# Convolution of the recurrent layer in four blocks of up to 344 tokens in place of five of 256, its runs dealt unevenly over the groups of the recursion

## The chip, the cores and the metric

The kernel runs on one core of a Trainium2 chip. The core has a matrix engine (PE, with its weight loads listed as PEld), a vector engine (DVE), an activation engine (ACT), a general engine (POOL) and an engine that only issues transfers (SP). Each engine takes its instructions in the order in which they were written down for it, and an instruction that waits holds up all that stand behind it on that engine. Data moves between DRAM, the on-chip memory and the accumulators in PSUM; a transfer is issued by an engine, most often SP, and lands some microseconds later.

The metric is the time of one execution on the device in microseconds (us), as a median of several runs. Each profile is of one execution.

## The reference, cut to what matters

The program is a backbone of two layers over 1024 latent tokens and 256 context tokens, 1024 features each. The even layer is the one that matters here. Its mixer has two halves of 512 features: a short gated convolution, and a recurrence (RWKV-7) that runs over the tokens in both directions.

```python
def conv3(u, w):
    up = jnp.pad(u, ((0, 0), (1, 1), (0, 0)))
    return up[:, :-2] * w[0] + up[:, 1:-1] * w[1] + up[:, 2:] * w[2]

def conv_branch(u, gate_b, gate_c):
    return gate_b * conv3(gate_c * u, conv_w)

def step(S, inp):                      # one token of the recurrence
    rt, wt, kt, vt, kkt, at = inp
    sa = jnp.einsum('bhij,bhj->bhi', S, -kkt)
    S = S * wt[:, :, None, :] + sa[..., None] * (kkt * at)[:, :, None, :] + vt[..., :, None] * kt[:, :, None, :]
    return S, jnp.einsum('bhij,bhj->bhi', S, rt)

p_lat = _split(h_lat @ w_in, EVEN_SPLIT)     # u, gate_b, gate_c: three projections of 512 features for the convolution
out_lat = jnp.concatenate([conv_branch(*p_lat[0:3]), rwkv_readout(...)], axis=-1) @ w_out
```

The convolution sees three neighbouring tokens; the context and the latent tokens are padded apart. So it is, in the main, three matrix products of (1280 tokens x 1024) by (1024 x 512), followed by a few elementwise operations.

## The kernel before

The work runs in stages, one after the other: the norm and projections of the even layer, the recursion of the recurrence with the convolution woven into it (`even_scan`), the output projection, an expert stage, the odd layer and a second expert stage. The change lies in the recursion's stage, with one edit in the stage ahead of it.

**Tokens in the recursion.** The 1280 tokens are cut into 20 pieces of 64, two pieces to a group, so there are ten groups, 0 to 9, and both directions advance together. For each group the kernel runs four generators, each of which issues some instructions and yields:

- `preps`, two groups ahead: loads of the inputs (tiles `s`, `ln`, `lr`, `lb`, `lk`), exponentials on ACT, products on DVE (tiles `AR`, `BK`), products on PE into `pr` (line 724, transposes line 738), which DVE masks into `PB` (line 728). Part of `PB` is stored to DRAM as `Ld` (line 735).
- `inverse`, one group ahead: loads `iW` from `Ld` (line 747) and runs 62 DVE operations in turn (lines 756 and 760, tiles `itmp` and `iG`); then it stores `iG` to DRAM as `Gd` in eight transfers (line 766) and loads it in another layout as `TT` in four (line 773).
- `merge`: DVE transposes `TT` into `Z` (line 782); PE multiplies twice (lines 788 and 796), with ACT copies between. The first of these products, `pu<-Z,PB` on line 788, is called the merge below.
- `serials`: two recursion steps for the two pieces of 64. PE products `X<-UV,PB` (line 819), `X<-S,AR` (826), `pu<-X,TT` (839), `pu<-UV,BT` (847), with ACT copies between, and the update of the state `S` on DVE (849, 850). A step needs the state of the one before.

**The convolution** (`conv`) is a fifth generator. For every block of 256 tokens it loads the split inputs `cvhh` and `cvhl` (line 626, one buffer each, so a block's load waits for the last product of the block before). For each of four feature blocks f it makes the three projections. A projection is two chunks; a chunk is one weight load `cvw` of 512 KB (line 641, three buffers) and 12 products of 256 columns (line 643), and then a yield. So a block has 24 chunks and the whole convolution 120. After the three projections of a feature block, ACT, DVE and POOL apply the gate and the three taps (tiles `cvu`, `cvg`, `cvx`, lines 634 to 658). What the next block needs of its left neighbour is kept in `keep`.

**What sets the order.** Each group's generators are dealt out by `interleave`, each with a number of runs and the stretch of the group in which they fall. The convolution has `NCV` = 10 runs in each of the twelve turns (-2 to 9). That is the order in which instructions are written; a scheduler in the language then places them on each engine by its own estimate of when they can start, so that a chunk may move to a place well ahead of its turn. The 12 products of a chunk are mostly kept together (`burst`).

**Ahead of the recursion** `keep()` in `even_project` stores the split inputs to DRAM (`hTD`), block by block, alternating with transfers of another generator.

Of the kernel before, what the change touches and what calls it, by code (L numbers as in the profile page):

```python
# [22 lines left out]
LT = LC + LL  # L23
# [30 lines left out]


N0, N2, N3 = 101, 1.0, .5
NCV = 10
NA = 4


# [120 lines left out]
class Kern:  # L181
# [252 lines left out]
    def even_project(self):  # L434
        nc, tc, I = self.nc, self.tc, self.I
        W = I["ev_w_in"][0]
        dp = self.dp
# [5 lines left out]
        with ExitStack() as es:  # L443
            P = lambda n, b, **k: es.enter_context(tc.tile_pool(name=n, bufs=b, **k))
            pp = P("pp", 3, space=PSUM)
            p2 = P("pp2", 2, space=PSUM)
            wp, hp = P("w", 2, side="right"), P("hT", 1, side="right")
            hT = [hp.tile([128, 8, LT], FR, name="hT" + x) for x in "hl"]
            with ExitStack() as e2:
                P2 = lambda n, b, **k: e2.enter_context(tc.tile_pool(name=n, bufs=b, **k))  # L450
                xp, sp, aw, ar = P2("hx", 4), P2("hs", 4), P2("haw", 3), P2("har", 2)
                self.even_hidden(hT, xp, sp, aw, ar, p2, P2("hps", 2, space=PSUM))
            self.hTD = [dp.tile([LT // 256, 128, 8, 256], FR, name="hTD" + x) for x in "hl"]

            def keep():
                for b in range(LT // 256):
                    for i in range(2):
                        nc.sync.dma_start(self.hTD[i][b].bitcast(FT), hT[i][:, :, b * 256:(b + 1) * 256].bitcast(FT))
                        yield

            p3 = P("pp3", 2, space=PSUM)
# [155 lines left out]
    def conv(self, P):  # L617

        nc = self.nc
        hp, wp, cp, c1, pp = P("cvh", 1), P("cvw", 3), P("cvt", 2), P("cv1", 1), P("cvp", 1, space=PSUM)  # L620
        keep = c1.tile([128, 4, 3], FT, name="keep")
        yield
        for b in range(LT // 256):
            h = [hp.tile([128, 8, 256], FR, name="cvh" + x) for x in "hl"]
            for i in range(2):
                nc.sync.dma_start(h[i].bitcast(FT), self.hTD[i][b].bitcast(FT))
            if b < 2:
                nc.gpsimd.memset(keep, 0.0)
            for f in range(4):

                u = cp.tile([128, 259], FT, name="cvu", bufs=1)
                g = cp.tile([128, 257], FT, name="cvg", bufs=1)
                t = cp.tile([128, 257], FT, name="cvx", bufs=1)
                nc.gpsimd.tensor_copy(u[:, 0:2], keep[:, f, 0:2])
                nc.gpsimd.tensor_copy(g[:, 0:1], keep[:, f, 2:3])
                nc.gpsimd.memset(u[:, 258:259], 0.0)
                for i, dst in enumerate((u[:, 2:258], g[:, 1:257], None)):
                    ps = pp.tile([128, 256], FT, name="cvp")
# [8 lines left out]
                    if dst is not None:  # L647
                        nc.scalar.activation(dst, ps, AF.Copy)
                nc.vector.tensor_tensor(u[:, 2:258], u[:, 2:258], ps, OP.mult)
                cw = lambda i: self.pcv("conv", 1, 4 * i + f)  # L650
                nc.scalar.activation(t, u[:, 0:257], AF.Copy, scale=cw(0))
                for i in (1, 2):
                    nc.vector.scalar_tensor_tensor(t, u[:, i:i + 257], cw(i), t, op0=OP.mult, op1=OP.add)
                nc.vector.tensor_tensor(t, t, g, OP.mult)
                x, y = (1 if b < 2 else 0), (257 if b in (0, LT // 256 - 1) else 256)
                nc.sync.dma_start(self.mixD[f, :, 256 * b - 1 + x:256 * b - 1 + y], t[:, x:y])
                nc.gpsimd.tensor_copy(keep[:, f, 0:2], u[:, 256:258])
                nc.gpsimd.tensor_copy(keep[:, f, 2:3], g[:, 256:257])

    def even_scan(self, P0):  # L660

# [8 lines left out]
        with es:  # L670
# [201 lines left out]
            for g in range(-2, NG):  # L872
                jobs = [(n, a, b, f(q)) for n, a, b, f, q in
                        ((2, 0.25, 0.4, merge, g), (4, 0.45, 1.2, serials, g), (15, 0.1, 1.05, inverse, g + 1),
                         (10, -0.3, 0.65, preps, g + 2)) if 0 <= q < NG]
                jobs.append((NCV, 0.0, 1.0, islice(conv, NCV)))
                if g > 7:

                    n = 31 if g == 8 else 10
                    jobs.append((n, 0.0, 1.0, islice(readout, n)))  # L880
                interleave(jobs)
# [1018 lines left out]
```

## Time and profile before

| | us |
|---|---|
| median of 3 runs | 4136.39 (4134.12 to 4136.67) |
| the profiled execution | 4126.59 |
| its span, first to last instruction | 4124.8 |
| recursion's stage, first convolution product to first output projection | 357 to 951 |
| mean granted PE clock over the span | 0.938 of full speed |

The page of the profile gives the busy time of each engine; the windows give the same for stretches of the span, with the granted PE clock as a share of full speed (2.4 GHz; the lower level is 1.2 GHz, 0.5 of it). The timeline gives single instructions with the idle time of the engine just before and what ended it. The chain of what ended last could be followed back only as far as 2347 us in this trace, so the recursion's stage has to be read from waits, windows and timeline.

Both timelines and windows count from the span's start. The first product of each merge stands at 456.6, 501.0, 548.9, 602.5, 650.2, 702.2, 753.1, 803.4, 853.8 and 909.9 us.

### The profile page before, as it was taken

The page shows a single profiled execution, that of the slowest core. Times are in us where ns is not written, and L with a number is a line of the kernel's source. Part 1 is how long each engine was busy: PE and PEld are TensorE (multiplying, and loading weights), DVE is VectorE, ACT ScalarE, POOL GpSimd, SP SyncE. Part 2 cuts the span into 40 slices and gives each one's busy share as a digit, 9 for nine tenths or more (in the row PEclk, how much of TensorE's full clock was granted, in tenths as well). Part 3 has the DMA queues.
Part 4 walks back from the last instruction along what each step waited for, and adds up shares of the span by engine and source line. Part 5 has one row for each costly group of instructions (what it writes and reads, how often), then busy time and mean ns, then how long its engine had stood idle before and what let it go on. Part 6 is the DMA issues. An engine that isn't in the chain of part 4 may idle for free. (4 is left out here: it accounts for less than half of the span.)

```text
span 4124.8 us, 66207 instructions
## 1 busy us (share of the span) xinstructions
PE 3737.1 (91%) x25578; PEld 2852.8 (69%) x25578; DVE 2764.9 (67%) x3906; ACT 2162.9 (52%) x3058; POOL 695.6 (17%) x682
## 2 busy tenths in 40 slices
PE   7989787868789999999999798998799499999998
PEld 5757787757556666666666565787467388888887
DVE  4255666764468777777777641465554599999997
ACT  4422222222246666666666431453555288878876
POOL 2101111242211010101010311452421210001010
PEclk9999899979889999999999899998799699999999
DMA  8988877756558787887878536223432699999997
GB/s 278 330 249 282 250 246 225 232 165 217 194 195 308 263 305 283 285 300 269 298 273 291 166 118 187 84 83 118 128 115 81 236 373 379 377 380 380 380 382 249
DMA packets 674650, 1026.25 MB, mean 249 GB/s; under 512 B 97089, under 2 KB 285537, under 8 KB 672542
## 3 DMA queue, kind: packets, MB, share of 16 engines
q1 hardware_dynamic: 657790, 963.22, 67.9%
q0 software_dynamic: 11360, 39.92, 3.7%
q10 hardware_dynamic: 5184, 18.88, 1.2%
q8 instruction: 201, 3.29, 0.3%
q14 instruction: 115, 0.94, 0.1%
HBM read 906.29 MB, written 115.60 MB: 248 GB/s over the span
## 5 line engine op out<-in xcount | busy, mean ns | idle before, releaser
L348 DVE TENSOR_TENSOR wl<-w,wh 128x1024 fp32r<-128x1024 f32 x1140 | 1356.0, 1221 | 134.9 <-ACT wh L347 105.4
L347 ACT ACTIVATE wh<-w 128x1024 fp32r<-128x1024 f32 x1152 | 1213.4, 1060 | 307.5 <-PE p L1115 251.5
L1115 PE MATMUL p<-wh,xh 128*128 128x512 f32 x1536 | 612.5, 399 | 0.0
L1115 PE MATMUL p<-wl,xh 128*128 128x512 f32 x1536 | 601.2, 391 | 0.2
L1115 PE MATMUL p<-wh,xl 128*128 128x512 f32 x1536 | 600.4, 391 | 0.0
L1115 PEld LDWEIGHTS p<-wh,xh 128*128 128x128 f32 x1536 | 289.6, 189 | 71.0 <-issue 13.4
L1115 PEld LDWEIGHTS p<-wl,xh 128*128 128x128 f32 x1536 | 289.3, 188 | 63.1 <-DVE wl L348 1.0
L1115 PEld LDWEIGHTS p<-wh,xl 128*128 128x128 f32 x1536 | 289.8, 189 | 57.2 <-DVE xl L348 0.4
L1115 PE MATMUL p<-wh,hh 128*128 128x512 f32 x768 | 307.9, 401 | 0.0
L1115 PE MATMUL p<-wl,hh 128*128 128x512 f32 x768 | 300.0, 391 | 0.3 <-DVE wl L348 0.2
L1115 PE MATMUL p<-wh,hl 128*128 128x512 f32 x768 | 299.8, 390 | 0.0
L353 PE MATMUL pj<-hTh,wchh 128*128 128x512 f32 (+1 forms) x720 | 279.2, 388 | 2.0 <-ACT wchh L347 1.1
L353 PE MATMUL pj<-hTl,wchh 128*128 128x512 f32 (+1 forms) x720 | 273.5, 384 | 5.2 <-DVE hTl L348 3.4
L353 PE MATMUL pj<-hTh,wchl 128*128 128x512 f32 (+1 forms) x720 | 276.9, 385 | 0.5 <-DVE wchl L348 0.5
L643 PE MATMUL cvp<-cvhh,cvw 128*128 128x256 f32 x960 | 207.2, 315 | 59.1 <-DMA cvw<-cwD 42.4
L643 PEld LDWEIGHTS cvp<-cvhh,cvw 128*128 128x128 f32 x960 | 165.1, 211 | 70.7 <-DMA cvw<-cwD 43.9
L1125 PE MATMUL pc<-w,xc 128*32 128x512 f32 x1536 | 174.7, 595 | 0.0
L1115 PEld LDWEIGHTS p<-wh,hh 128*128 128x128 f32 x768 | 144.1, 188 | 42.5 <-issue 13.4
L1115 PEld LDWEIGHTS p<-wl,hh 128*128 128x128 f32 x768 | 144.2, 188 | 32.7 <-DVE wl L348 1.1
L353 PEld LDWEIGHTS pj<-hTh,wchh 128*128 128x128 f32 x720 | 138.2, 192 | 38.8 <-issue 10.1
L353 PEld LDWEIGHTS pj<-hTl,wchh 128*128 128x128 f32 x720 | 136.6, 191 | 39.6 <-issue 10.8
L1115 PEld LDWEIGHTS p<-wh,hl 128*128 128x128 f32 x768 | 144.4, 188 | 27.8
(417 smaller groups left out, 6335.9 us busy)
## 6 DMA issues: line engine op xcount, KB each, us to landing
w<-in_moe_w_dram SPq DMA_DIRECT2D x576, 1024.0 KB
cvw<-cwD SPq DMA_DIRECT2D x120, 512.0 KB
adaw<-in_ada_w_dram SPq DMA_DIRECT2D x80, 512.0 KB
wch<-in_od_w_in_dram SPq DMA_DIRECT2D x38, 512.0 KB
cwD<-cvs SPq DMA_DIRECT2D x24, 512.0 KB
bias<-in_rpbt_dram SPq DMA_DIRECT2D x48, 192.0 KB
xt<-in_x_dram SPq DMA_DIRECT2D x16, 512.0 KB
adaw<-in_ada_w_dram SPq DMA_DIRECT2D x8, 1024.0 KB
```

Source lines behind the costliest of these rows:

```text
L347: self.nc.scalar.activation(hi, src, AF.Copy)
L348: (eng or self.nc.vector).tensor_tensor(lo, src, hi.bitcast(FT), OP.subtract)
L353: self.nc.tensor.matmul(ps, a[x], b[y], start=start and i == 0, stop=stop and i == 2, **kw)
L643: self.burst((lambda k=k, i=i, x=x, y=y: nc.tensor.matmul(ps, hl[:, x, k], h[y][:, k0 + k], start=k0 + k == 0 and i == 0, stop=k0 + k == 7 ...
L1115: self.keep(nc.tensor.matmul(ps[i], a[u], w[0][k][v], start=first and k == 0 and j == 0, stop=last and k == 3 and j == 2))
L1125: self.keep(nc.tensor.matmul(pc[32 * g:32 * g + 32], x[2][:, kt + kk, :], ws[g % 2][1][:, kk], start=n == 0 and k == 0, stop=n == len(stag ...
```

## The change

The blocks become (start, tokens) = (0, 256), (256, 344), (600, 344), (944, 336). The weight chunks stay as they are, so there are 96 in place of 120, and a product has 344 or 336 columns in place of 256 except in the context block. The runs per turn become six in the first five turns, seven in the next five, then 12 and 19. The small copies between blocks go from POOL to ACT and DVE and are made only where a next block needs them.

```diff
-NCV = 10
+NCV = [6] * 5 + [7] * 5 + [12, 19]
+CB = ((0, 256), (256, 344), (600, 344), (944, 336))
...
-            self.hTD = [dp.tile([LT // 256, 128, 8, 256], FR, name="hTD" + x) for x in "hl"]
+            self.hTD = [[dp.tile([128, 8, n], FR, name=f"hTD{x}{b}") for b, (_, n) in enumerate(CB)] for x in "hl"]
...
-                        nc.sync.dma_start(self.hTD[i][b].bitcast(FT), hT[i][:, :, b * 256:(b + 1) * 256].bitcast(FT))
+                        nc.sync.dma_start(self.hTD[i][b].bitcast(FT), hT[i][:, :, b0:b0 + n].bitcast(FT))
...
-        for b in range(LT // 256):
-            h = [hp.tile([128, 8, 256], FR, name="cvh" + x) for x in "hl"]
+        for b, (b0, n) in enumerate(CB):
+            h = [hp.tile([128, 8, big], FR, name="cvh" + x)[:, :, :n] for x in "hl"]
...
+            first, last = b < 2, b in (0, len(CB) - 1)
...
-                nc.gpsimd.tensor_copy(u[:, 0:2], keep[:, f, 0:2])
-                nc.gpsimd.tensor_copy(g[:, 0:1], keep[:, f, 2:3])
-                nc.gpsimd.memset(u[:, 258:259], 0.0)
+                nc.scalar.activation(u[:, 0:2], keep[:, f, 0:2], AF.Copy)
+                nc.scalar.activation(g[:, 0:1], keep[:, f, 2:3], AF.Copy)
+                if last:
+                    nc.gpsimd.memset(u[:, n + 2:n + 3], 0.0)
...
+                    elif i == 1:
+                        nc.scalar.activation(g[:, 1:n + 1], ps, AF.Copy)
+                        if not last:
+                            nc.scalar.activation(keep[:, f, 2:3], g[:, n:n + 1], AF.Copy)
...
-                nc.gpsimd.tensor_copy(keep[:, f, 0:2], u[:, 256:258])
-                nc.gpsimd.tensor_copy(keep[:, f, 2:3], g[:, 256:257])
+                if not last:
+                    nc.vector.tensor_copy(keep[:, f, 0:2], u[:, n:n + 2])
...
-                jobs.append((NCV, 0.0, 1.0, islice(conv, NCV)))
+                jobs.append((NCV[g + 2], 0.0, 1.0, islice(conv, NCV[g + 2])))
```

Line numbers in the changed kernel are higher by 5 to 10 in these functions (643 becomes 648, 788 becomes 798).

Three places show how the order of the engines changes. The first is SP's queue around the load of `TT` for group 3: `cvw` are the convolution's weights, `iW`, `Gd` and `TT` belong to the inverse, `yD` to a recursion step. Before:

```order
L641 DMA cvw<-cwD 128x1024
L747 DMA iW<-Ld 64x1024
L766 DMA Gd<-iG 16x16x32 x8
L773 DMA TT<-Gd 32x16x32 x4
L747 DMA iW<-Ld 64x1024
L694 DMA ln<-nkD 128x512
L694 DMA lr<-rD 128x512
L694 DMA ln<-nkD 128x512
L694 DMA lr<-rD 128x512
L656 DMA mixD<-cvx 128x256
L641 DMA cvw<-cwD 128x1024 x3
```

And in the changed kernel:

```order
L646 DMA cvw<-cwD 128x1024
L757 DMA iW<-Ld 64x1024
L776 DMA Gd<-iG 16x16x32 x8
L783 DMA TT<-Gd 32x16x32 x2
L866 DMA yD_2854<-Y 64x512
L866 DMA yD_2855<-Y 64x512
L783 DMA TT<-Gd 32x16x32 x2
L757 DMA iW<-Ld 64x1024
L822 DMA UV_5627<-vD 64x512
L822 DMA UV_5628<-vD 64x512
L646 DMA cvw<-cwD 128x1024 x3
```

In both, the weights for the next chunks stand behind the stores and loads of the inverse; before, 62 of the 120 weight loads are issued ahead of this `TT`, now 53 of the 96.

The second place is PE at a boundary between blocks of the convolution, where the first products of a new block need the inputs just loaded. Before, the boundary that stands at a merge is the one into the fourth block, at the merge of group 4:

```order
L738 MATMUL pr<-cst,BK 128x128 x4
L826 MATMUL X_6697<-S,AR 64x64 x2
L724 MATMUL pr<-AR,BK 128x128 x8
L643 MATMUL cvp<-cvhh,cvw 128x256 x2
L788 MATMUL pu<-Z,PB 32x32 x32
L724 MATMUL pr<-AR,BK 128x128 x8
L796 MATMUL pu<-TT,Z 32x32
L643 MATMUL cvp<-cvhl,cvw 128x256
```

In the changed kernel it is the one into the third block, ahead of the merge of group 2. The chunk's first two products stand ahead of products of the recursion and of `pr`, and of these rows the second begins the other ten products, which also stand ahead of the merge:

```order
L648 MATMUL cvp<-cvhh,cvw 128x344 x2
...
L734 MATMUL pr<-AR,BK 128x128 x7
...
L648 MATMUL cvp<-cvhl,cvw 128x344
...
L748 MATMUL pr<-cst,BK 128x128 x8
...
L798 MATMUL pu<-Z,PB 32x32 x32
L734 MATMUL pr<-AR,BK 128x128 x8
```

Before, two products of the new block are ahead of that merge, in the changed kernel all 12.

The third place is PE at the start of the ninth merge (group 8) before, with the chunks of the convolution beside it:

```order
L643 MATMUL cvp<-cvhl,cvw 128x256
L788 MATMUL pu<-Z,PB 32x32 x32
L724 MATMUL pr<-AR,BK 128x128 x8
L643 MATMUL cvp<-cvhh,cvw 128x256 x2
```

And the merge of group 7 in the changed kernel, after which no product of the convolution comes any more:

```order
L734 MATMUL pr<-AR,BK 128x128 x7
L798 MATMUL pu<-Z,PB 32x32 x32
L734 MATMUL pr<-AR,BK 128x128
L806 MATMUL pu<-TT,Z 32x32
L734 MATMUL pr<-AR,BK 128x128 x7
```

Counted on PE, the chunks that stand ahead of the merges of groups 0 to 9 are 30, 42, 52, 65, 72, 83, 95, 105, 116 and 120 before, and 29, 40, 49, 58, 70, 76, 88, 96, 96 and 96 in the changed kernel. The scheduler has moved the runs that the table deals to the last two turns to places ahead of the merge of group 7.

## Rows read from the trace of the kernel before

**Rows 1.** The page: busy time, share of the span, instructions; then one issue group.

```profile
PE 3737.1 (91%) x25578; PEld 2852.8 (69%) x25578; DVE 2764.9 (67%) x3906; ACT 2162.9 (52%) x3058; POOL 695.6 (17%) x682
...
cvw<-cwD SPq DMA_DIRECT2D x120, 512.0 KB
```

**Rows 2.** Windows: busy us (count) per engine, PE clock, DMA share, GB/s.

```profile
357.00:453.80 96.80, 77.91 (x683) 69.36 (x682) 62.30 (x152) 20.20 (x40) 13.08 (x43) 0.90 0.90 291
...
453.80:803.00 349.20, 291.83 (x5039) 267.40 (x5038) 227.32 (x642) 98.00 (x205) 53.34 (x158) 0.92 0.77 236
...
803.00:853.80 50.80, 41.11 (x654) 36.42 (x653) 36.40 (x90) 14.01 (x29) 20.00 (x31) 0.87 0.76 225
853.80:909.90 56.10, 36.90 (x616) 30.78 (x616) 39.73 (x90) 14.14 (x30) 22.64 (x23) 0.71 0.49 132
```

**Rows 3.** Waits, 350 to 950 us: waited for; total us, times, longest.

```profile
POOL cvu L634 <- DVE cvx L653: 31.2, 12, 5.5
...
PE cvp L643 <- DMA cvw<-cwD: 42.4, 22, 6.2
...
PE cvp L643 <- DMA cvhh<-hTDh: 12.7, 3, 8.8
```

**Rows 4.** Timeline of SP ahead of one merge: start, us, what.

```profile
727.70 3.42 SPq L766 DMA_DIRECT2D Gd<-iG  x7
731.22 3.27 SPq L773 DMA_DIRECT2D TT<-Gd  x4
...
737.78 0.88 SPq L641 DMA_DIRECT2D cvw<-cwD  x2
```

**Rows 5.** Timeline of DVE and PE at the same merge, idle time before in brackets.

```profile
726.00 0.19 DVE L760 TENSOR_TENSOR iG<-iG,itmp 128x16 f32<-128x16 f32 x1
...
743.64 0.79 PE L643 MATMUL cvp<-cvhh,cvw 128*128 128x256 f32 x2 [5.44 <-DMA cvw<-cwD]
745.09 0.63 PE L643 MATMUL cvp<-cvhh,cvw 128*128 128x256 f32 x2
...
745.73 0.63 PE L643 MATMUL cvp<-cvhh,cvw 128*128 128x256 f32 x2
...
753.15 1.04 PE L788 MATMUL pu<-Z,PB 32*32 32x32 f32 x54
...
753.25 0.69 DVE L728 TENSOR_TENSOR PB<-pr,cst 128x512 f32<-128x512 f32 x1 [8.04 <-PE pr L724]
```

**Rows 6.** Timeline of PE: products of 256 and of 512 columns in a stream.

```profile
361.17 0.40 PE L643 MATMUL cvp<-cvhh,cvw 128*128 128x256 f32 x2
...
361.53 0.40 PE L643 MATMUL cvp<-cvhh,cvw 128*128 128x256 f32 x2
...
350.98 0.40 PE L353 MATMUL pj<-hTh,wchh 128*128 128x512 f32 x1
351.21 0.39 PE L353 MATMUL pj<-hTh,wchl 128*128 128x512 f32 x1
```

**Rows 7.** Timeline of SP and PE at a block boundary, and at an earlier one.

```profile
641.84 0.43 SPq L626 DMA_DIRECT2D cvhh<-hTDh  x1
642.31 0.46 SPq L626 DMA_DIRECT2D cvhl<-hTDl  x1
...
649.44 0.80 PE L643 MATMUL cvp<-cvhh,cvw 128*128 128x256 f32 x2 [8.77 <-DMA cvhh<-hTDh]
...
654.26 0.58 PE L643 MATMUL cvp<-cvhl,cvw 128*128 128x256 f32 x1
```

**Rows 8.** Windows of the convolution's own instructions (`cvp`) alone, same columns.

```profile
803.00:853.80 50.80, 22.14 (x134) 19.67 (x132) 0.84 (x2) 1.54 (x4) 0.87 0.76 225
853.80:909.90 56.10, 8.06 (x48) 7.14 (x48) 0.42 (x1) 0.39 (x1) 0.71 0.49 132
```

**Rows 9.** Timeline of DVE and PE in the last groups, idle time before in brackets.

```profile
834.60 0.69 DVE L917 TENSOR_REDUCE m<-lr 128x8 f32<-128x512 f32 x1 [4.99 <-POOL lr L914]
...
909.93 1.92 PE L788 MATMUL pu<-Z,PB 32*32 32x32 f32 x64 [10.37 <-DVE Z L782]
```

More of the change, by code (lines that the diff above doesn't have):

```diff
@@ L619, in conv @@
         nc = self.nc
-        hp, wp, cp, c1, pp = P("cvh", 1), P("cvw", 3), P("cvt", 2), P("cv1", 1), P("cvp", 1, space=PSUM)
+        hp, wp, cp, c1, pp = P("cvh", 1), P("cvw", 3), P("cvt", 1), P("cv1", 1), P("cvp", 1, space=PSUM)
         keep = c1.tile([128, 4, 3], FT, name="keep")
+        big = max(n for _, n in CB)
         yield
-        for b in range(LT // 256):
-            h = [hp.tile([128, 8, 256], FR, name="cvh" + x) for x in "hl"]
+        for b, (b0, n) in enumerate(CB):
+            h = [hp.tile([128, 8, big], FR, name="cvh" + x)[:, :, :n] for x in "hl"]
             for i in range(2):
                 nc.sync.dma_start(h[i].bitcast(FT), self.hTD[i][b].bitcast(FT))
-            if b < 2:
+            first, last = b < 2, b in (0, len(CB) - 1)
+            if first:
                 nc.gpsimd.memset(keep, 0.0)
             for f in range(4):
-                u = cp.tile([128, 259], FT, name="cvu", bufs=1)
-                g = cp.tile([128, 257], FT, name="cvg", bufs=1)
-                t = cp.tile([128, 257], FT, name="cvx", bufs=1)
-                nc.gpsimd.tensor_copy(u[:, 0:2], keep[:, f, 0:2])
-                nc.gpsimd.tensor_copy(g[:, 0:1], keep[:, f, 2:3])
-                nc.gpsimd.memset(u[:, 258:259], 0.0)
-                for i, dst in enumerate((u[:, 2:258], g[:, 1:257], None)):
-                    ps = pp.tile([128, 256], FT, name="cvp")
+                u = cp.tile([128, big + 3], FT, name="cvu")
+                g = cp.tile([128, big + 1], FT, name="cvg")
+                t = cp.tile([128, big + 1], FT, name="cvx")
+                nc.scalar.activation(u[:, 0:2], keep[:, f, 0:2], AF.Copy)
+                nc.scalar.activation(g[:, 0:1], keep[:, f, 2:3], AF.Copy)
+                if last:
+                    nc.gpsimd.memset(u[:, n + 2:n + 3], 0.0)
+                for i in range(3):
+                    ps = pp.tile([128, big], FT, name="cvp")[:, :n]
                     for k0 in (0, 4):
@@ L646, in conv @@
                         yield
-                    if dst is not None:
-                        nc.scalar.activation(dst, ps, AF.Copy)
-                nc.vector.tensor_tensor(u[:, 2:258], u[:, 2:258], ps, OP.mult)
+                    if i == 0:
+                        nc.scalar.activation(u[:, 2:n + 2], ps, AF.Copy)
+                    elif i == 1:
+                        nc.scalar.activation(g[:, 1:n + 1], ps, AF.Copy)
+                        if not last:
+                            nc.scalar.activation(keep[:, f, 2:3], g[:, n:n + 1], AF.Copy)
+                nc.vector.tensor_tensor(u[:, 2:n + 2], u[:, 2:n + 2], ps, OP.mult)
+                m = n + last
                 cw = lambda i: self.pcv("conv", 1, 4 * i + f)
-                nc.scalar.activation(t, u[:, 0:257], AF.Copy, scale=cw(0))
+                nc.scalar.activation(t[:, :m], u[:, 0:m], AF.Copy, scale=cw(0))
                 for i in (1, 2):
[L653 to L656, printed above, removed]
-                nc.gpsimd.tensor_copy(keep[:, f, 0:2], u[:, 256:258])
-                nc.gpsimd.tensor_copy(keep[:, f, 2:3], g[:, 256:257])
+                    nc.vector.scalar_tensor_tensor(t[:, :m], u[:, i:i + m], cw(i), t[:, :m], op0=OP.mult, op1=OP.add)
+                nc.vector.tensor_tensor(t[:, :m], t[:, :m], g[:, :m], OP.mult)
+                x = 1 if first else 0
+                nc.sync.dma_start(self.mixD[f, :, b0 - 1 + x:b0 - 1 + m], t[:, x:m])
+                if not last:
+                    nc.vector.tensor_copy(keep[:, f, 0:2], u[:, n:n + 2])
     def even_scan(self, P0):
```

## The prediction

> **What bounds the kernel now.** I began with the page: PE is busy 91% of the span [rows 1], which looks like a matrix-bound program. But the change touches one stage, so the windows of that stage come next [rows 2]. In the first of them, up to the first merge, the transfers are the tighter resource (DMA share 0.90, PE 77.91 of 96.80 us). In the seven groups after it PE is busy 291.83 of 349.20 us: 57 us idle in all, some 8 us per group, so neither PE nor DVE (227.32 us) fills the time. There I asked for waits [rows 3]. The convolution waits 42.4 us in 22 places for its weights and 12.7 us in 3 for its inputs.
>
> The timelines at one merge [rows 4, 5] show why a group takes as long as it does. DVE ends the inverse at 726.00 us. SP then stores `Gd` (727.70) and loads `TT` (731.22), and only behind those issues the next `cvw` (737.78). The weights land at 743.64, 5.9 us later, and PE, which is in order, has stood idle 5.44 us. It then runs three chunks, with products of the recursion and of `pr` between, and reaches the merge at 753.15. DVE has stood idle 8.04 us for `pr` at 753.25. So between two merges there is a loop: an inverse on DVE, the trip through DRAM, the weight landing, then what PE does from there to the merge. A chunk that PE must do in this last part is on the path; a chunk at any other place lies beside the inverse. Where the chunks stand decides, more than how many there are.
>
> After 803 us it is different. In the group before the ninth merge DVE is busy 36.40 of 50.80 us, and in the one after it 39.73 of 56.10 [rows 2]; DVE waits 4.99 us for POOL, and the tenth merge waits 10.37 us for `Z` from DVE [rows 9]. PE is not the bound there.
>
> **The change part by part.** All terms are in us; minus is faster.
>
> *T1, the stream on PE.* Columns are the same before and after: 1440 products x 256 = 368,640 = 288 x 256 + 576 x 344 + 288 x 336. Three products of 256 columns take 361.53 − 361.17 = 0.36, so 0.120 each; one of 512 columns takes 351.21 − 350.98 = 0.23 [rows 6]. A line through both gives 0.43 ns a column and about 10 ns a product; 344 columns are 0.158, 336 columns 0.154. A chunk of 12 products is then 1.44, 1.89 or 1.85, and 120 x 1.44 = 172.8 becomes 24 x 1.44 + 48 x 1.89 + 24 x 1.85 = 169.7. That is −3.1, and at most that (bounds −4 and 0), since PE idles beside it.
>
> The Trainium skill ("TensorE: Matmul & The Clock Gate", section "Back-to-back issue gap") gives a warm gap of columns/2.4 plus about 2.5 ns: 109 ns for 256 columns, where the row has 120. By it 288 products fewer would save 0.7 and not 3.1; the measured spacing decides here.
>
> *T2, chunks on the loop.* From the two orders I counted, for each merge, the chunks whose weights are issued behind that group's `TT` and that PE does ahead of the merge. For groups 0 to 9: before 0, 3, 1, 3, 0, 3, 3, 3, 1, 0, which is 17; in the changed kernel 0, 3, 0, 5, 4, 1, 4, 3, 0, 0, which is 20. Two of the five at merge 3 stand beside a recursion step, so I count 18. At full clock 17 x 1.44 = 24.5 becomes 18 x 1.88 = 33.8: +9.3. The lower bound is 0, when the wider chunks only fill what is left of the idle time. The upper bound is the half clock: behind the 5.44 us stall products of 256 columns come at 745.73 − 745.09 = 0.64 for three, 0.21 each, not 0.12 [rows 5]. If 13 of the slots ran so, 13 x 12 x (0.28 − 0.21) = 11 more beside the wider columns, and another landing for the fourth and fifth chunk of a merge (three buffers) adds 2.1 (5.9 less the 3.8 that two chunks last) a few times: +26. I take +9.3, since before about half of the slots already show the low clock and the difference in width, 0.44 a chunk, is the safe part.
>
> *T3, the loads at block boundaries.* There is one buffer, so a block's inputs are issued when the last product of the block before is done: 641.84 and 642.31, first used at 649.44 and 654.26, thus 7.6 and 12 later, with PE idle 8.77 [rows 7]. The new loads are 1.376 MB and not 1.0, times 344/256 = 1.344: 10.2 and 16.1 if all of it scales. Before, one of three late boundaries stands at a merge and puts two products there. In the changed kernel the boundary into the third block puts all 12 products ahead of merge 2: +5 (bounds 0, since PE has other rows between, and +9). The boundary into the fourth block comes in the middle of a recursion step: +2. The one gone from merge 4: −4. Sum +3, bounds −3 and +12.
>
> The Trainium skill ("DMA: Bandwidth & Descriptors", section "Anatomy of one DMA — SWDGE (gpsimd) path") fits 2.0 us plus bytes/436e3 for a transfer issued by GpSimd; these are issued by SP and the row has 7.6 in place of the 4.4 that the fit gives. By its slope a larger load is 0.8 later, not 2.6, and T3 would be some 2 smaller; no row of before has a load of this size in this place.
>
> *T4, the last groups.* Before, 11 chunks stand after the merge at 803 us (22.14 us of PE) and four after the next (8.06 us) [rows 8]. The changed kernel has none after merge 7. For group 7 PE's 41.11 us fall to 19. The group is then bounded by DVE: 36.40 plus its waits, about 45 where it was 50.80, −5. But the next group shows the other side: with four chunks it takes 56.10, at a granted clock of 0.71 against 0.87 [rows 2], because the recursion's own products run slower there. Group 8 gains little, since DVE and POOL set it [rows 9], and group 9 has no chunk before either. I take −5, bounds −15 and +6.
>
> *T5, up to the first merge.* 24 chunks of 1.44 and 5 of 1.89 make 44.0 where 30 of 1.44 make 43.2; the stage has a DMA share of 0.90 [rows 2], so the place of the first weight loads, which now stand behind stores of the recursion's inputs, counts more than PE: +1, bounds −5 and +6.
>
> *T6, small copies.* POOL loses about 90 copies and memsets; it waits 31.2 us over 12 places at the convolution's `cvu` copy [rows 3]. The copies of `u` and `g` from `keep` move to ACT, behind which the recursion's copies of `X`, `UV` and `Z` products stand; if the tile is not free, ACT waits there in POOL's place, up to 5.5 a time. DVE gets eight copies of 0.2 at most and loses 16 wider operations with the fewer blocks. The cover is that buffers alternate; if it is gone, eight waits of an average 2.6 cost +20, of which few would stand at a recursion step. I take +1, bounds −3 and +8.
>
> The sum is −3.1 + 9.3 + 3 − 5 + 1 + 1 = +6.2. The profiled execution (4126.59: span 4124.8 and 1.8 around it) lies 9.8 below the median 4136.39, so with this sum that execution would be 4132.8; I put the difference on the median: 4142.6. A difference of 0.2%, 8.3 us, is about what a measurement of this kernel can tell from none, so the forecast is no change that can be told, on its slow side.
>
> **The rivals.**
>
> *Faster.* The wider chunks at the loop are swallowed by the 5.44 us waits: a chunk of 1.88 keeps PE supplied longer per load, and 24 loads fewer are queued on SP. T2 is 0, T3 is 0, the last groups give −14 (group 7 and 8 both come down to DVE's busy time and 5 us of waits). With T1 and T5, T6 as above that is −3.1 − 14 + 2 = −15, so 4121. For it: 57 us of PE idle in the middle [rows 2], POOL's waits gone. Against it: that idle lies where PE waits for a landing, and work done after the landing can't fill it.
>
> *Slower.* At merges 3, 4 and 6 the five, four and four chunks stand behind one `TT`. There are three weight buffers, so the fourth waits for the first chunk to end and then a landing, and after each such stall the products come at half clock [rows 5]. T2 is +22, T3 +8, T4 −5, T5 and T6 +4, T1 −3: +26, so 4162. It decides as soon as more than about three of the 18 slots are stretched in that way. For it: every merge of before where three chunks stand behind the `TT` shows a stall. Against it: such slots partly lie beside a recursion step, and a later merge gives the next loop less to wait for.
>
> *The change doesn't do what its table says.* The table deals 12 and 19 runs to the last two turns; the order of PE shows none after merge 7. This is in the sum already: the last turns are free of the convolution, and merges 3 to 7 carry what they would have had. So I don't price it apart.
>
> **How the numbers follow.** I give the forecast (within 8.3 us of the median, 4128 to 4145) 0.36, the faster rival and its kin 0.30, the slower 0.34. The ends for 8 in 10: below, the faster rival with a little more from its tail, 4117; above, the slower with two more from the loads, 4164. The likeliest case's own range is 4132 to 4150: T2 between +3 and +16.
>
> **What would show it.** T1: `cvp` products spaced 0.158 at full clock. T2: the waits of `cvp` for `cvw` at 30 to 55 us; chunks at half clock after the stalls at merges 3, 4 and 6, and those groups about 2 to 4 longer than before, where merges 2 and 5 are shorter. T3: a wait for `cvhh` or `cvhl` of about 10 just ahead of merge 2. T4: merge 7 to merge 8 about 45 against 50.4, merge 8 to 9 near 54, and a granted clock near 0.7 in both. T6: POOL's waits for `cvx` at `cvu` gone and not more than 10 us of such waits on ACT. The whole: the first output projection some 6 us later than 951. It is wrong if the stages after the recursion differ by more than 5 us, if PE at the merges waits for something that isn't the weights (the `Z` of DVE, say) in the middle groups too, or if the last groups get longer for want of the clock.

## The result, and the profile after

The changed kernel takes 4169.93 us (median of 4 runs, 4166.40 to 4175.14) against 4136.53 us before (4134.12 to 4137.60): a ratio of 1.0079, interval 1.0063 to 1.0096. It is 33 us slower, and outside the predicted range of 4117 to 4164. The profiled execution took 4172.68 us.

The loss lies in the recursion's stage. The first output projection starts at 992.4 us, 41.6 later than the 950.8 before, and the execution before that was profiled is itself 10 below its median. The windows of the changed kernel, cut at the first convolution product, the first merge and the merges of groups 7, 8 and 9 (columns as in [rows 2], whose first cut lies 2.8 us ahead of the first merge at 456.6):

```profile
359.50:464.70 105.20, 83.97 (x668) 74.73 (x668) 61.19 (x156) 19.61 (x45) 2.01 (x13) 0.87 0.85 275
464.70:851.30 386.60, 323.01 (x4927) 287.64 (x4926) 234.67 (x633) 104.56 (x230) 43.21 (x103) 0.89 0.67 197
851.30:891.90 40.60, 28.86 (x492) 22.55 (x492) 27.27 (x82) 10.65 (x20) 6.46 (x11) 0.71 0.48 118
891.90:950.70 58.80, 33.30 (x598) 25.88 (x597) 38.29 (x85) 14.19 (x31) 25.96 (x23) 0.67 0.42 107
```

The seven groups in the middle, from the first merge to that of group 7, take 386.6 us where they took 346.8 (456.6 to 803.4). DVE does about the same work in them (234.67 us, and 227.32 in the slightly longer window of [rows 2]), so it is idle some 30 us more. The first merge is 8.1 later, the group after merge 7 is 9.8 shorter, the next 2.7 longer.

PE has more to do in these seven groups. The windows of the convolution's own instructions (`cvp`, columns as in [rows 8]), before and then changed:

```profile
456.60:803.40 346.80, 136.77 (x901) 123.08 (x900) 5.42 (x13) 9.63 (x25) 0.92 0.78 237
```

```profile
464.70:851.30 386.60, 159.86 (x805) 138.52 (x804) 6.11 (x12) 10.01 (x22) 0.89 0.67 197
```

There are 67 chunks there in place of 75, but 43 of them have 344 columns and 24 have 336, so that the convolution takes 23.1 us more of PE. Behind merge 7, where it took 30.0 us before, it takes nothing now, and the time from there to the projection fell by 6.3 us only (147.4 and 141.1).

The waits of the stage (waited for; total us, times, longest), the lines that answer to [rows 3]:

```profile
POOL cvu L641 <- DVE cvx L663: 64.3, 4, 27.4
...
PE cvp L648 <- DMA cvw<-cwD: 42.1, 12, 9.7
...
DVE cvu L658 <- PE cvp L648: 33.6, 11, 12.0
...
ACT cvu L638 <- DVE cvx L663: 19.8, 13, 3.4
...
PE cvp L648 <- DMA cvhh<-hTDh: 17.4, 2, 10.8
```

PE waits as long for weights as before (42.1 and 42.4 us), in 12 places and not 22. New is that DVE waits 33.6 us for the product that it multiplies in the convolution. Two of DVE's waits for PE between 397 and 960 us, before and then changed:

```profile
DVE PB L728 <- PE pr L724: 56.4, 13, 9.4
...
DVE cvu L649 <- PE cvp L643: 8.2, 9, 2.6
```

```profile
DVE PB L738 <- PE pr L734: 60.5, 18, 14.4
DVE cvu L658 <- PE cvp L648: 33.6, 11, 12.0
```

**The gap between two inverses.** DVE runs one inverse after another: 62 operations, then a stretch in which it does other work and waits until the next inverse starts. I call this stretch the gap (from the last `iG` of one to the first `itmp` of the next, from DVE's timeline). The ten inverses and nine gaps fill the stage from about 397 us to the end of the tenth inverse. Gaps after groups 0 to 8, in us:

| | 0 | 1 | 2 | 3 | 4 | 5 | 6 | 7 | 8 | gaps | inverses |
|---|---|---|---|---|---|---|---|---|---|---|---|
| before | 12.0 | 23.8 | 13.4 | 14.4 | 11.7 | 14.4 | 12.4 | 20.9 | 14.7 | 137.7 | 350.4 |
| changed | 16.5 | 25.4 | 27.7 | 32.3 | 22.9 | 13.7 | 21.4 | 25.4 | 12.2 | 197.5 | 324.9 |

So the gaps are 59.8 longer and the inverses 25.5 shorter. Start and tail add 0.5 and 6.8, which makes the 41.6. DVE does other work, and waits, among the operations of an inverse too. Summed from its timeline, its idle time in the gaps rose from 75.5 to 132.2 us and that inside the inverses fell from 77.0 to 55.5: the waits of `PB` moved out of the inverses (34 us there, now 13) into the gaps (22, now 47), and their sum is nearly the same. Gaps and inverses have to be taken together. Then DVE idles 35 us more, and 25 of them are its wait for the convolution's product (8.2 and 33.6).

The longest is the gap of group 3. DVE's timeline in the changed kernel:

```profile
593.66 0.19 DVE L770 TENSOR_TENSOR iG<-iG,itmp 128x16 f32<-128x16 f32 x1
...
601.25 0.69 DVE L717 TENSOR_TENSOR AR<-ln,E 128x512 f32<-128x512 f32 x1 [4.97 <-PE X L836]
...
615.73 0.51 DVE L658 TENSOR_TENSOR cvu<-cvu,cvp 128x344 f32<-128x344 f32 x1 [11.99 <-PE cvp L648]
...
624.94 1.29 DVE L738 TENSOR_TENSOR PB<-pr,cst 128x512 f32<-128x512 f32 x2 [3.78 <-PE pr L734]
626.14 0.18 DVE L766 TENSOR_TENSOR itmp<-iW,iG 128x31 f32<-128x31 f32 x1
```

And what it waits for, on SP and PE:

```profile
594.24 5.60 SPq L776 DMA_DIRECT2D Gd<-iG  x8
...
607.00 1.53 SPq L646 DMA_DIRECT2D cvw<-cwD  x3
```

```profile
611.82 0.94 PE L648 MATMUL cvp<-cvhh,cvw 128*128 128x344 f32 x2 [9.75 <-DMA cvw<-cwD]
```

The weights stand behind the inverse's stores on SP, PE stalls on them, and DVE, in order, can't start the next inverse: the multiplication of the convolution and the `PB` masks of the group after next stand ahead of it. The same gap before:

```profile
575.80 0.19 DVE L760 TENSOR_TENSOR iG<-iG,itmp 128x16 f32<-128x16 f32 x1
...
589.23 1.29 DVE L728 TENSOR_TENSOR PB<-pr,cst 128x512 f32<-128x512 f32 x2 [2.52 <-PE pr L724]
590.44 0.18 DVE L756 TENSOR_TENSOR itmp<-iW,iG 128x31 f32<-128x31 f32 x1
```

### The profile page after: what moved, and what is told of

Its sections match the earlier page's. It is cut to its first block, busy times and chain, and to the rows that moved or that the text cites. A ratio compares the mean times of both kernels' runs of the same rounds, so it can differ in the third digit from the quotient of the medians.

```text
span 4170.9 us, 65467 instructions
## 1 busy us (share of the span) xinstructions
PE 3766.1 (90%) x25290; PEld 2868.5 (69%) x25290; DVE 2765.2 (66%) x3898; ACT 2168.4 (52%) x3086; POOL 671.8 (16%) x590
## 4 chain that ended last, share of the span: by engine, by line
PE 68%; DVE 5%; DMA 5%; issue 3%; ACT 2%; POOL 2%; SPq 1%; POOLq 0%; ACTq 0%; DVEq 0%
PE p L1125 37%; PE pj L354 6%; PE pc L1135 6%; PE po L354 5%; PE cvp L648 2%; PE pt L1160 1%; PE pt L1095 1%; PE oT L1722 1%; PE tp L1002 1%; PE o L1539 1%; PE pr L734 1%; PE z L1519 1%; DVE iG L770 1%; DVE itmp L766 1%; DMA cvw<-cwD 1%
## 5 line engine op out<-in xcount | busy, mean ns | idle before, releaser
L1125 PEld LDWEIGHTS p<-wh,xh 128*128 128x128 f32 x1536 | 289.6, 189 | 70.8 <-issue 13.4
L648 PE MATMUL cvp<-cvhh,cvw 128*128 128x344 f32 (+2 forms) x768 | 199.3, 348 | 62.6 <-DMA cvw<-cwD 42.1
L648 PEld LDWEIGHTS cvp<-cvhh,cvw 128*128 128x128 f32 x768 | 141.8, 211 | 72.5 <-DMA cvw<-cwD 39.9
L1125 PEld LDWEIGHTS p<-wh,hh 128*128 128x128 f32 x768 | 144.2, 188 | 42.5 <-issue 13.4
L1125 PEld LDWEIGHTS p<-wh,hl 128*128 128x128 f32 x768 | 144.5, 188 | 27.7
```

The costliest lines, as they stand in the source:

```text
L648: self.burst((lambda k=k, i=i, x=x, y=y: nc.tensor.matmul(ps, hl[:, x, k], h[y][:, k0 + k], start=k0 + k == 0 and i == 0, stop=k0 + k == 7 ...
L1125: self.keep(nc.tensor.matmul(ps[i], a[u], w[0][k][v], start=first and k == 0 and j == 0, stop=last and k == 3 and j == 2))
```

## The experiments

The table holds all 18 runs: the median against the kernel before measured beside it, and from one profiled execution the start of the first output projection and the sums of gaps and inverses. Single executions of the kernel before lay between 4120 and 4149 us, so a difference of some 10 us in the right half is not a finding.

| run | us | ratio (interval) | projection | gaps | inverses |
|---|---|---|---|---|---|
| before | 4134 to 4138 | | 950.8 | 137.7 | 350.4 |
| changed | 4169.93 | 1.0079 (1.0063 to 1.0096) | 992.4 | 197.5 | 324.9 |
| e1 new copies, five blocks | 4158.89 | 1.0058 (1.0043 to 1.0073) | 955.9 | 138.8 | 357.3 |
| e2 copies on POOL | 4161.85 | 1.0068 (1.0051 to 1.0085) | 985.4 | 196.5 | 323.3 |
| e3 even deal | 4175.59 | 1.0095 (1.0078 to 1.0111) | 1004.9 | 210.6 | 319.0 |
| e4 uneven deal alone | 4145.23 | 1.0024 (1.0012 to 1.0036) | 978.2 | 160.3 | 357.2 |
| e5 inputs once | 4187.43 | 1.0131 (1.0109 to 1.0153) | 989.7 | 210.7 | 308.8 |
| e6 weights once | 4129.32 | 0.9996 (0.9982 to 1.0011) | 952.0 | 161.8 | 309.4 |
| e7 weights once, before | 4146.46 | 1.0033 (1.0016 to 1.0049) | 970.0 | 163.6 | 334.3 |
| e8 inputs issued by ACT | 4185.26 | 1.0124 (1.0102 to 1.0146) | 996.1 | 202.1 | 324.6 |
| e9 weights issued by POOL | 4200.33 | 1.0152 (1.0121 to 1.0183) | 1006.1 | 194.5 | 331.9 |
| e10 weights issued by ACT | 4163.07 | 1.0059 (1.0034 to 1.0084) | 984.1 | 183.1 | 320.2 |
| e11 no gate and taps | 4171.03 | 1.0079 (1.0048 to 1.0111) | 992.8 | 214.9 | 320.0 |
| e12 before, four weight buffers | 4161.09 | 1.0068 (1.0037 to 1.0099) | 968.0 | 178.0 | 315.3 |
| e13 chunks kept, 14 and 8 | 4169.65 | 1.0073 (1.0054 to 1.0093) | 992.9 | 209.7 | 309.2 |
| e14 chunks kept, own table | 4174.22 | 1.0095 (1.0071 to 1.0118) | 995.5 | 184.9 | 304.8 |
| e15 before, chunks kept | 4162.16 | 1.0058 (1.0035 to 1.0082) | 988.0 | 195.3 | 316.5 |
| e16 preps later | 4132.52 | 0.9986 (0.9976 to 0.9996) | 941.3 | 160.3 | 305.1 |
| e17 before, preps later | 4125.31 | 0.9975 (0.9963 to 0.9987) | 950.4 | 135.2 | 339.3 |
| e18 preps later, 0.85 | 4127.85 | 0.9977 (0.9964 to 0.9989) | 948.3 | 161.1 | 309.6 |

**Parts of the change: e1 to e4.** e1 is the changed code with five blocks:

```diff
-CB = ((0, 256), (256, 344), (600, 344), (944, 336))
+CB = tuple((256 * b, 256) for b in range(5))
-NCV = [6] * 5 + [7] * 5 + [12, 19]
+NCV = [10] * 12
```

> The changed kernel with five blocks of 256 and ten runs a turn, so that only the new copies on ACT and DVE are left of the change; the chunks stand exactly where they stand in the kernel before. Theory S (the longer blocks are the cost, through the places that the chunks and block inputs take): 4137 +- 5. Rival C (the copies on ACT hold back the recursion's copies): 4155 or more. Theory D (the uneven deal): 4137, as S.

The total misses S, but not in the way of C: in the stage it loses 5.1 us, its gaps are those of before, and most of its loss comes after it. From the projection to the first `sl` product of the odd layer it takes 1959.4 us (before 1946.6), and 20 more are lost behind that. Nothing was edited there; the scheduler put loads of the odd layer in another order. So a total may hold a loss that isn't the stage's, and from here on the stage is read by the projection.

e2 puts the copies back (`nc.gpsimd.tensor_copy` for the four `keep` copies).

> The changed kernel with the four small copies back on POOL; the chunks stand where they do in the changed kernel. S: 4165 to 4172, no gain. C: back to 4145 or less. D: as S.

Some 6 us come back (7 in the stage), a little below the range of S; 28 of the 33 remain with the same places of the chunks. The intervals of e2 and of the changed kernel overlap. The copies are a small part at most.

e3 is `NCV = [8] * 12`, e4 the kernel before with `NCV = [7, 8, 7, 8, 8, 9, 9, 9, 9, 8, 15, 23]`.

> The changed kernel with eight runs in every turn in place of the uneven table. The chunks ahead of the merges of groups 0 to 9 are 28, 40, 49, 58, 70, 77, 88, 96, 96, 96 (changed kernel 29, 40, 49, 58, 70, 76, 88, 96, 96, 96), nearly the same. S: 4165 to 4175. C: as S. D: 4140 or less.

> The kernel before with its 120 runs dealt unevenly (7 to 9 in the first ten turns, then 15 and 23). Chunks behind the load of TT at merges 0 to 9: 0, 3, 1, 3, 1, 1, 1, 3, 0, 0. S: 4125 to 4138, no loss, since fewer chunks stand on the loop than before. C: 4137. D: 4155 or more.

With the longer blocks an even deal is no better: the scheduler moves the chunks anyway. The deal alone costs 11 us where S had none: a five-block kernel loses too when its chunks stand elsewhere. Its gap of group 3 is 25.7 us, and with 76 chunks the convolution takes 146.1 us of PE in the seven middle groups (before 136.8).

**Waits taken away: e5 to e8.** e5 loads the inputs of one block and uses them for all four. e6 (changed kernel) and e7 (kernel before) load the weights of two chunks and use them for all (`if k0 not in W1:` ahead of the load). So these three leave out the other loads. e8 has `nc.scalar.dma_start` for the inputs and leaves out nothing.

> The changed kernel, but the block inputs cvhh and cvhl are loaded once and serve all four blocks, which leaves out the inputs of blocks 2 to 4: no wait at a block boundary. Chunks behind the load of TT at merges 0 to 9: 1, 5, 5, 4, 4, 3, 1, 0, 0, 0, more than in the changed kernel. Theory H (the boundary load at group 2 and what stands behind it costs most): first output projection 992 -> 970 or less. Theory S (chunks that stand behind weight loads issued after TT cost most): 985 to 1000.

> The changed kernel, but the weights of the first two chunks serve all 96, which leaves out the other 94 weight loads: no product waits for weights, the boundaries stay. S: first output projection 992 -> 950 or less. H: 975 or more, as the boundary's wait stays.

> The kernel before with the weights of the first two chunks for all 120. S: it loses the same waits, 951 -> 920 or less, and stands within 8 of the changed kernel without the loads, so that the difference of 41 in this stage is gone. H: it gains as well, but the changed kernel without the loads stays 15 or more behind it.

> The changed kernel with the block inputs' loads issued by ACT and not by SP, nothing left out. Chunks behind TT at merges 0 to 9: 0, 3, 1, 3, 2, 3, 4, 0, 0, 0 (two fewer at merges 3 and 4 than in the changed kernel). H: the load starts as soon as the block before is done and not behind Gd and TT; the wait of 10.8 falls to 7 or less, first output projection 992 -> 978. S: 992 -> 975, through merges 3 and 4. Neither: 985 or more.

H falls: without any boundary wait the projection starts at 989.7, and e8, with 996.1, gains nothing either. e6 gives nearly all back, as S said, but e7 gains nothing and loses 19, against S. The chunks move as well, to 64 in the seven middle groups in e6 (138.7 us of the convolution on PE) and to 84 in e7 (155.5). So the two runs don't tell the loads from the places of the chunks.

**The weights' queue and DVE's share: e9 to e12.** e9 and e10 have `nc.gpsimd.dma_start` and `nc.scalar.dma_start` for `cvw`, e11 leaves out the gate and taps and stores the third projection alone, e12 has `P("cvw", 4)` in the kernel before.

> The changed kernel with its 96 weight loads issued by POOL and not by SP; nothing is left out, and no weight load stands behind Gd and TT any more. Theory S (the weights wait on SP behind the inverse's transfers, PE stalls, and the products pr that DVE's queue waits for stand behind the stall): the idle stretches of DVE between two inverses, 197.5 in all, fall to 165 or less, as they did (161.8) with no weight loads at all; first output projection 992 -> 960 to 970. Rival P (any new placing of the work costs the kernel some 20 to 40, whatever the weights do): 980 or more. Of the total only the stage counts, since in this kernel the scheduler also places the odd layer's loads otherwise.

> The changed kernel with its 96 weight loads issued by ACT. S: as with POOL, if ACT's own work isn't held up by the wait for a free weight buffer; that wait stands ahead of the recursion's copies on ACT, so less is won: first output projection 970 to 980. P: 980 or more.

> The changed kernel without the gate and the three taps of the convolution (the third projection alone is stored), so that DVE does nothing for the convolution. Chunks behind TT at merges 0 to 9: 0, 3, 4, 1, 4, 1, 3, 3, 0, 0. S: the waits of DVE for the convolution's products (27 in the six gaps of groups 1 to 6) go, but those for pr, which stand behind the same stalled chunks on PE, take most of their place: gaps 197.5 -> 180 to 195, first output projection 992 -> 975 to 985. Theory V (DVE's own queue is what is blocked by the multiplication): gaps 170 or less, 992 -> 960.

> The kernel before with four weight buffers in place of three. Chunks behind TT at merges 0 to 9: 2, 3, 0, 5, 0, 4, 0, 3, 0, 0. S: one more chunk is there before the stall, but as many chunks stand behind TT as before (17): gaps 137.7 -> 125 to 145, first output projection 940 to 955. P: 970 or more.

PE's waits for weights in the stage, in e9 and then e10 (same columns as above), are a third of what they were:

```profile
PE cvp L648 <- DMA cvw<-cwD: 13.1, 10, 5.5
```

```profile
PE cvp L648 <- DMA cvw<-cwD: 12.4, 7, 5.4
```

Yet the stage ends at 1006.1 and 984.1. So S falls as a theory of the weights alone, though e9 is not clean: issuing costs POOL, which is busy 78 us in the seven middle groups and not 43. V falls with e11: DVE then waits for other products of the same late PE, and the gaps are 214.9. Only the gap of group 3 does what V said (32.3 to 19.0); those of groups 4 and 5 grow to 30.6 and 31.3, and 72 chunks stand in the middle groups. e12, with four weight buffers, loses 25 us although its chunks behind `TT` are as many as before: S had 940 to 955 for the projection, P 970 or more, and it starts at 968.0.

**The order held: e13 to e15.** The first product of a chunk is kept in program order, as the other eleven are:

```diff
-        next(steps)()
+        if first == "keep":
+            self.keep(next(steps)())
...
+        else:
+            next(steps)()
```

for the convolution alone, with `NCV = [14, 14] + [8] * 8 + [3, 1]` in e13, the change's table in e14, ten a turn and five blocks in e15.

> The changed kernel with its chunks held in the order in which they are written (the scheduler may not move them to another turn) and dealt 14, 14, then 8 a turn, then 3 and 1. Chunks ahead of the last PB product before the next inverse whose weights are issued behind the stores of the inverse just ended: -1, -2, 0, -2, -2, -1 for the gaps of groups 1 to 6 (changed kernel 1, -1, 3, 2, -1, 2). Theory G (DVE alternates between an inverse and a gap, and a gap is long as soon as one such chunk stands ahead of PB): the gaps of groups 2 to 6 fall to 11 to 16 each, all gaps from 197.5 to 145 or less, first output projection 992 -> 950 or less, total 4140 or less. Rival P (any placing other than that of the kernel before costs 20 to 40): gaps 180 or more, first output projection 975 or more.

> The changed kernel with its chunks held in the order in which they are written, in its own table (six, seven, then 12 and 19): the last two turns really get the chunks that the table deals to them. Chunks at merges 0 to 9: 14, 20, 26, 32, 39, 46, 53, 60, 66, 82. Counted as above, -2 for the gaps of groups 1 to 5 and 0 for that of group 6. G: the gaps of groups 1 to 6 are 11 to 16 each; but 14 chunks (26 us) come after the last merge, where PE has little else to hide behind; first output projection 950 to 970. P: 975 or more, gaps 180 or more.

> The kernel before with its chunks held in the order in which they are written, ten a turn. Chunks at merges 0 to 9: 24, 33, 42, 53, 63, 72, 83, 93, 103, 113; counted as above, 1, -1, -1, -2, -1, 1 for the gaps of groups 1 to 6 (before 1, -1, 0, -2, 0, 0). G: about as before, the gap of group 6 some 9 longer, those of 2 to 5 at 11 to 15, seven chunks (10 us) after the last merge; first output projection 950 to 965. P: 970 or more.

By the count in its expectation no chunk with late weights stands ahead of `PB` in e13, and still its gaps of groups 1 to 6 are 22 to 25 us. What PE waits for has only changed its name:

```profile
PE X L835 <- DMA UV<-vD: 39.1, 11, 6.8
...
PE cvp L654 <- DMA cvw<-cwD: 8.2, 5, 3.3
```

`UV` is an input of a recursion step, loaded on the same queue. So the form of G that counts such chunks is wrong, and up to here the rival P holds: every five-block kernel in an order of its own lost, too (e4, e12 and e15: 11, 25 and 26 us). e14 shows what the table as written would do: inverses and gaps take 490 us, as before (488) and 32 less than in the changed kernel, but after the last merge 14 chunks are left, and the projection starts at 995.5. So where the scheduler puts the chunks does count in the loop.

**What stands ahead of the next inverse: e16 to e18.** One number is changed, in the changed kernel (e16, e18 with 0.85) and in the kernel before (e17):

```diff
-                         (10, -0.3, 0.65, preps, g + 2)) if 0 <= q < NG]
+                         (10, -0.2, 0.8, preps, g + 2)) if 0 <= q < NG]
```

In DVE's order four `PB` masks fewer now stand ahead of the starts of inverses 2 to 8.

> The changed kernel with the preps dealt from -0.2 to 0.8 of a turn and not -0.3 to 0.65. On DVE the start of the next inverse then stands ahead of the last four PB products that stood ahead of it (PBs ahead of inverses 2 to 8: 24, 32, 40, 48, 56, 64, 72 in place of 28, 36, 44, 52, 60, 68, 76), so that a late pr doesn't hold up the next inverse. Theory G (the loss is DVE's gap between inverses, made long by PB products that stand behind late PE work): gaps of groups 2 to 6 fall from 14 to 32 to 10 to 16, all gaps from 197.5 to 150 or less, first output projection 992 -> 965 or less. Rival R (PE is late as a whole; DVE then waits as long elsewhere): gaps and inverses together stay above 510 (changed kernel 522, before 488), first output projection 980 or more.

> The kernel before with the preps dealt from -0.2 to 0.8 of a turn. G: its gaps of groups 2 to 6 are short already (11.7 to 14.4); that of group 1 falls from 23.8 to 16; gaps and inverses together 475 to 490, first output projection 940 to 955. R: 505 or more, first output projection 970 or more, like every other five-block kernel in a new order (968 to 988).

> As e16 with the preps dealt from -0.2 to 0.85. The chunks stand where they do in e16, the recursion's order differs at a few places, and in the odd layer the scheduler leaves the loads of bias, nq and nV where the kernel before has them (in e16 seven of them stood elsewhere). Theory G with O (the order of the odd layer's loads costs e16 some 12): first output projection 938 to 950, first sl product of the odd layer to the first output projection as before (1947), total 4117 to 4127, below both kernels. Without O: 4130 to 4138 as e16. Rival R: 4150 or more.

In e16 the projection starts at 941.3, 51 us earlier than in the changed kernel; gaps and inverses take 465 us and not 522. The total is 4132.52, the loss is gone. R and P fall: a new order need not cost anything. G's numbers for single gaps were too good: of groups 2 to 6 only the last is in the range (17.6, 25.1, 23.6, 17.7 and 14.9), together they give 19 us, groups 0 and 1 give 20, and the sum is 160.3 and not 150. Another 20 come from the inverses, which G didn't mention. DVE's two longest waits in e16 between 397 and 920 us:

```profile
DVE itmp L766 <- DMA iW<-Ld: 44.4, 8, 11.8
DVE PB L738 <- PE pr L734: 30.3, 13, 8.0
```

`PB` is down from 60.5 to 30.3, and what is late next is the load of the inverse itself. In the gap of group 3 DVE waits 7.98 in one place for `pr` and then does other work, and starts the inverse after a wait of 1.81:

```profile
554.90 1.45 DVE L738 TENSOR_TENSOR PB<-pr,cst 128x512 f32<-128x512 f32 x2 [7.98 <-PE pr L734]
...
569.19 0.19 DVE L766 TENSOR_TENSOR itmp<-iW,iG 128x31 f32<-128x31 f32 x1 [1.81 <-DMA iW<-Ld]
```

e16 gives 16 us back in the odd layer, whose loads its scheduler moved: from the projection to the first `sl` product it takes 1962.3 us (before 1946.6). In e18, with the odd layer in the order of before, this is 1944.3:

```profile
948.28 1.22 PE L354 MATMUL po<-woh,mxh 128*128 128x512 f32 x2 [7.25 <-ACT mxh L348]
...
2892.55 1.65 PE L1670 MATMUL sl<-nk,nq 64*128 64x384 f32 x4 [14.97 <-DMA nq<-nqD]
```

e18 takes 4127.85 us, 10 below the kernel before and 42 below the changed kernel, just above its expected range. e17 takes 4125.31, also 10 below before, but in its stage nothing is won: gaps and inverses fall from 488 to 475, as G said, the time behind them grows by as much, and the projection starts at 950.4 as before. Its gap of group 1 falls to 9.9, and that of group 3 grows to 25.6, which G did not have. The blocks of 344 and those of 256 thus end within 3 us of each other, and within the intervals neither is better.

The number moves the chunks as much as the masks. Between the merges of groups 0 and 7, and from there to the projection:

| run | chunks in the seven groups | the convolution on PE there, us | the seven groups, us | merge 7 to projection, us |
|---|---|---|---|---|
| before | 75 | 136.8 | 346.8 | 147.4 |
| changed | 67 | 159.9 | 386.6 | 141.1 |
| e13 | 58 | 131.0 | 374.7 | 150.8 |
| e14 | 46 | 109.0 | 360.6 | 188.7 |
| e15 | 69 | 130.9 | 371.0 | 153.3 |
| e16 | 50 | 120.7 | 326.8 | 168.8 |
| e17 | 63 | 112.4 | 322.3 | 168.2 |
| e18 | 50 | 120.7 | 329.8 | 170.7 |

In e17 the seven groups are 24.5 us shorter than before, and 24.3 us of the convolution have left them. In e16 they are 59.8 shorter than in the changed kernel, and 39.1 of the convolution have left them. So a rival to G stands: what counts is how much of the convolution lies in the loop. Against it as the only cause stand e13, e14 and e15, which have less of it there than the kernel before and still take 14 to 28 us longer; but they hold the chunks in the written order, which is a change of its own. No run here parts the two.

## Why the prediction was wrong, point by point

- **T1, the stream on PE: right.** The first products of two triples of 344 columns stand at 592.15 and 592.63, 0.16 a product; predicted 0.158. Over the stage the convolution takes 218.9 us of PE where it took 221.3. But "the same columns" holds for the stage and not for the seven middle groups, which have 23.1 us more.
- **T2, chunks on the loop: this step failed.** It counted the chunks behind `TT` and charged 0.44 us for the width of each, 9.3 in all; with T3 that is 12.3 for the middle groups, which are 39.8 longer. Its places are right in part: the groups up to merges 3, 4 and 6 are 8.0, 10.5 and 7.0 longer (forecast 2 to 4), that up to merge 5 is 5.9 shorter, and the waits of 42.1 us for weights lie in the predicted 30 to 55. But the groups up to merges 1 and 7, with as many such chunks as before, are 4.9 and 5.6 longer, and that up to merge 2, with fewer, is 9.7 longer. What the runs show in place of the price: the convolution takes 23.1 us more of PE in these groups, and DVE idles 35 us more in gaps and inverses, 25 of them in its wait for the convolution's product. The prediction had a term for neither. It saw that the middle groups carry the chunks of the last turns, held that this was in the sum already, and read the loop as one from the landing to the merge on PE, without asking what DVE has queued behind PE. The 8.04 us for `pr` in [rows 5] was a hint: that wait stands inside the next inverse (which starts at 738.64) and holds DVE's queue there.
- **T3, boundary loads: right in place, wrong as a cause.** PE waits 10.8 us for `cvhh` ahead of merge 2, as forecast, and that group is 9.7 longer where the term had +5. But e5, with no such wait, doesn't bring it back: that group takes 60.0 us in e5 and 57.6 in the changed kernel.
- **T4, the last groups: about right.** After merge 7 the group is 9.8 shorter (predicted 5), the next 2.7 longer where "little" was to be gained, at granted clocks of 0.71 and 0.67. Both effects of the term are there, in the sum −7.
- **T5, up to the first merge: too small.** The first merge is 8.1 later, predicted +1, just past the bound of 6. The start of inverse 0 moved only 0.5.
- **T6, small copies: in its bounds.** e2 puts it at some 6 us, near the upper bound of 8. The cover that the term names isn't there: `cvu`, `cvg` and `cvx` have one buffer each, before and after. The expected sign was wrong: POOL's waits for `cvx` didn't go (64.3 us at the copies' former neighbour, a memset), and ACT took 19.8 of its own, where I had at most 10.
- **The rivals.** The slower one (4162, chance 0.34) had the sign and nearly the size, and named merges 3, 4 and 6. That is luck in the main: its mechanism, slots at half clock and further landings on PE, isn't what the runs show. PE waited no longer for weights than before, and the slower slots made some 5 us. (This is an estimate: 67 chunks at T1's spacing would take 126 of the 159.9 us, the 75 before 108 of 136.8, so what the slower spacing adds went from 29 to 34.) That the table doesn't do what it says was right in itself; that it needs no price of its own is what failed. By e14, with the chunks where the table deals them, gaps and inverses are back at 490 us, and the loss lies behind the last merge.

What stays open: how the loss divides between the convolution's longer time in the loop and the place of `PB` ahead of the inverse. No run moved the `PB` masks alone: the number changed in e16 to e18 moves preps on every engine, the first inverse starts 7 us earlier, and 17 chunks leave the seven middle groups. That the masks' place is the cause is argued and not shown. For it speak two kernels with the longer blocks that recover, and e13 to e15, where fewer chunks alone did not help. Why e6 recovers and e9 and e10 don't was not tried further; without the loads the traffic between 460 and 850 us is also down from 197 to 117 GB/s.

## What to carry to other kernels

When work is woven into a loop over several in-order engines, count it by stretch of the loop and not over the whole stage: here the columns were the same in all, but 23 us more of the work on them stood in the loop, and the place that they had left gave only 6 us back. Then ask of each engine, not only of the busiest, what in its queue waits for that work; the wait that grew stood on DVE. Removing a wait that a profile names (block inputs, the engine's own operation) only showed the next one, and removing the waits for weights brought the stage back in one run of four (e6, not e7, e9 or e10). One number in the deal of another generator took 51 us out of the changed kernel's stage and nothing out of the stage before. Compare orders in stages that the edit doesn't touch before a total is put down to the edit.

## What had not been expected

The odd layer, some 1900 us behind the edit, changed its time by 16 us from the projection to its first `sl` product in e16 and 13 in e1, through the order of its loads, as far as e18 shows. The runs of one kernel spread by some 24 us (17 of the kernel before beside e18: 4124.31 to 4148.40), where the first three lay within 2.6.
